# The mixer's values by seven block products instead of eight, all of them behind the second head's queries

## The chip, the cores and the metric

The kernel runs on one core of a Trainium2 chip. The metric is the device time of one execution in microseconds (us), the median of several runs. TensorE (PE) multiplies matrices, VectorE (DVE) and ScalarE (ACT) work on elements, GpSimd (POOL) and SyncE (SP) here mostly issue transfers. Each engine carries out its own instructions in order; engines wait for each other by semaphores.

## The reference

One transformer layer in fp32, for 512 tokens of width 1024: a gated feed-forward part (FFN1), the token mixer, a second feed-forward part (FFN2) and a final norm. The change is inside the mixer, in the projection that makes `va` and `vb`:

```python
def token_mixer(h, w_in, w_out, lq1, lk1, lq2, lk2, subln_gain, rel_bias, layer):
    proj = h @ w_in                                   # 512 x 1024 by 1024 x 3072
    qa, ka, va, qb, kb, vb = jnp.split(proj, ..., axis=-1)   # 512 columns each
    ...
    oa = diff_attention(qa, ka, va, lam, rel_bias[:, :2 * N_DIFF_HEADS])   # 4 heads of 128
    oa = rmsnorm(oa, subln_gain) * (1.0 - lam0)
    ...
    ob = dilated_attention(qb, kb, vb, rel_bias[:, 2 * N_DIFF_HEADS:])     # 8 heads of 64
    mixed = jnp.concatenate([oa, ob], axis=-1)
    return mixed @ w_out

def diff_attention(q, k, v, lam, bias_table):
    ...                                               # two causal softmaxes per head
    a = p[:, :, 0] - lam * p[:, :, 1]
    return a @ v
```

`h` is the normed input of the mixer. The values of the four differential heads are `va`, those of the eight dilated heads `vb`.

## The kernel before, in words

**Products.** Every matrix product in fp32 is made of three products in a faster format: an operand is split into a high part (a cast, on ACT) and a low part (operand minus high, on DVE), and `mm3` (L177) adds high by high, low by high and high by low. A product instruction takes 128 columns of a stationary operand and up to 512 columns of a moving one. The normed input stands transposed in eight pieces of 128 rows, high `xh` and low `xl`; their second 256 tokens are made later than the first, so some names end in m (`xh7m`).

**Stages.** FFN1, then the mixer, then FFN2. In both feed-forward parts block products are already done by seven products for eight; in the mixer no product is. The mixer's work on PE is cut into chunks of about six products of 512 columns. Its eight units u are the four differential heads (u = 0 to 3) and the eight dilated heads in pairs (u = 4 to 7). A list `plan` (L1381) names the blocks of chunks in order: `q0` stands for the queries and keys of unit 0 (eight chunks), `w` for the values of the four differential heads (16 chunks, `wide_chunks`, L1455: 96 products of 512 columns), `v2` and `v3` for the values of pairs of dilated units (eight chunks each, `v_chunks`, L1430: 96 products of 256 columns each). The order is q0 q1 w q2 q3 q4 v2 q5 q6 v3 q7, and then the output projection `wo`.

**Attention between the chunks.** `attention(u, s)` (L1598) hangs a unit's other work on chunk numbers with `put(chunk, rank, function)`: from chunk s the eight scores (L1616 and L1617, two maps of four tiles), each followed by a reduction with bias and minimum on DVE (L1619) and an exponential on ACT (L1622), then the combination of the two maps (L1626 to L1642), the turned weights (`pt`, L1652 and L1707, copied to `ptx` by ACT), the products with the values (`po`, L1691 and L1719), norm, scale (L1742), a last turn (`ot`, L1748) and the high and low parts for `wo` (`mh`, `ml`, L1754 to L1765). `step(t)` runs what was hung on chunk t with a rank below 10, then the chunk's products, then the rest.

**What sets the order.** PE's order is written by hand: as `step` issues it. On DVE, ACT, POOL and SP a scheduler sets it from priorities in the same sequence of issue. Weights come with `load_w` (L163) through SP; `prep` and `ahead` (L1414 and L1424) queue their casts (L1406) and lows (L1410) some chunks ahead.

**PSUM banks.** Score results use two banks (tag `s`), the turned weights two (tag `t`), products four (tag `mm`).

**Direct units.** A unit's keys and queries are needed in both halves of the 128 partitions. For units in `DIRECT` ACT and DVE write both halves (`evac_now`); for the others SP copies the other half by transfers (`evac_k`, L1532).

Of the kernel before, what the change touches and what calls it, by code (L numbers as in the profile page):

```python
# [37 lines left out]
DIRECT = (0, 7)  # L38
# [5 lines left out]
EARLY_SLOTS = {(1, 0): ((19, 20), (14, 15)), (1, 1): ((23, 0), (26, 27))}  # L44

# [72 lines left out]
def tile_macaron(ctx: ExitStack, tc, xs, xT, wf, wgu1, wst1, wdg1, wqk, wvw, wv, wo, wgu2, wst2,  # L118
# [1274 lines left out]
    def unit(src, nm):  # L1393
        units.append((src, nm))
        return len(units) - 1

    loaded, ready, later = {}, {}, []

    def load(n):
        if n < len(units) and n not in loaded:  # L1400
            loaded[n] = load_w(*units[n])
            ready[n] = loaded[n][1:]
# [20 lines left out]
    def ahead(n):  # L1423
        prep(n + 2)  # L1424
        load(n + 3)
        return ready[n]
# [3 lines left out]
    def v_chunks(qr):  # L1430
        vi, hf = qr // 2, qr % 2
        us = [unit(wv[hf, c], f"v{qr}{c}") for c in range(2)]
        st = {}

        def chunk(c):
            i, kh = c // 2, c % 2
            if c == 0:
                ahead(us[0])
            if kh == 0:
                st["ps"] = mm_bank(f"pv{qr}{i}")  # L1440
            po = st["ps"][:, :256]
            wh, wl = ready[us[kh]]
            xs = slice(i * P, (i + 1) * P)
            for k in range(4 * kh, 4 * kh + 4):
                o = (k % 4) * 256
                T.matmul(po, xh[k][:, xs], wh[:, o:o + 256], start=k == 0, stop=False)
                T.matmul(po, xl[k][:, xs], wh[:, o:o + 256], start=False, stop=False)
                T.matmul(po, xh[k][:, xs], wl[:, o:o + 256], start=False, stop=k == KD - 1)
            if kh == 1:
                if hf == 0:  # L1450
                    vt[vi, i] = slot(vi * 4 + i, f"v{vi}{i}")
                A.copy(vt[vi, i][:, hf * 256:hf * 256 + 256], po)
            if c == 7:
                ahead(us[1])
        return [lambda c=c: chunk(c) for c in range(2 * NQ)]  # L1455

    def wide_chunks():


        us = [unit(wvw[c], f"vw{c}") for c in range(4)]  # L1460
        banks = []

        def chunk(c, i):
            if i == 0:
                ahead(us[c])
            if c == 0:
                banks.append(mm_bank(f"pvw{i}"))
            po = banks[i][:]
            wh, wl = ready[us[c]]
            xs = slice(i * P, (i + 1) * P)  # L1470
            for k in range(2 * c, 2 * c + 2):
                o = slice(k % 2 * S, (k % 2 + 1) * S)
                T.matmul(po, xh[k][:, xs], wh[:, o], start=k == 0, stop=False)
                T.matmul(po, xl[k][:, xs], wh[:, o], start=False, stop=False)
                T.matmul(po, xh[k][:, xs], wl[:, o], start=False, stop=k == KD - 1)
            if c == 3:
                vt[0, i] = slot(i, f"v0{i}")
                A.copy(vt[0, i][:], po)
        return [lambda c=c, i=i: chunk(c, i) for c in range(4) for i in range(NQ)]
# [4 lines left out]
    def qk_chunks(u):  # L1484
# [3 lines left out]
        def chunk(k):  # L1488
            if k == 0:
                st["pq"] = mm_bank(f"pq{u}")  # L1490
                st["pk"] = mm_bank(f"pk{u}")
            if u == 4 and k == 0:

                load(us[0] + 3)
                put(start["q4"] + 3, 10, prep, us[0] + 2)
            elif k % 4 == 0:
# [101 lines left out]
    def attention(u, s):  # L1598
# [178 lines left out]
        if diff:  # L1777

            step, tv = (2, s + 13) if u > 1 else (1, v_end[u] + 1 + 3 * u)
# [8 lines left out]
            put(e + 3 + (u > 1), 9 if u < 2 else 7, scale)  # L1788
# [11 lines left out]
        else:  # L1800
            tv = max(s + 9, v_end[u])
# [8 lines left out]
    for w in plan:  # L1810
        if w == "w":
            chunks += wide_chunks()
            continue
        chunks += (qk_chunks if w[0] == "q" else v_chunks)(int(w[1]))
        if w[0] == "q":
            attention(int(w[1]), len(chunks) + (8 if w[1] == "0" else 3 if w[1] == "7" else 5))
# [32 lines left out]
    put(9, 4, lam)  # L1849
    for n, c in enumerate((0, 0, 2)):  # L1850
        put(c, 0, load, n)
    for n, c in enumerate((3, 5)):
        put(c, 10, prep, n)
# [179 lines left out]
_INS = ["xs", "xT", "wf", "wgu1", "wst1", "wdg1", "wqk", "wvw", "wv", "wo", "wgu2", "wst2", "wdg2", "fg",  # L2033
# [95 lines left out]
```

## Time and profile before

| | before |
|---|---|
| median of 3 runs (lowest, highest) | 912.9 us (912.56 to 913.06) |
| profiled execution, from its first to its last instruction | 910.7 us |
| its mean granted TensorE clock | 0.998 |
| PE, weight loads, DVE, ACT, POOL busy | 99%, 90%, 81%, 62%, 11% |
| the mixer's first products; first products of w, of v2, of wo | 339.0; 363.9; 436.3; 519.3 us |

The profile gives no time of its own for the profiled execution beside its span of 910.7 us; the median of the runs is 2.2 us above that. A row of a group of instructions holds the program's line, the engine, the operation, output and inputs, the shapes, the count, the busy time, the mean time of one in ns, and the idle time of the engine just before with what ended it. In a timeline a row begins with the start and the duration in us. In a table by windows each engine has its busy us, with the number of its instructions in brackets, then the granted clock, the share of the transfer engines and GB/s.

### The profile page before, as it was taken

What the parts mean: (1) busy time and instruction counts of PE and PEld (TensorE: products, weight loads), DVE (VectorE), ACT (ScalarE), POOL (GpSimd) and SP (SyncE); (2) the same over time, 40 slices, a digit from 0 to 9 for tenths busy, and PEclk for the clock granted to TensorE, in tenths of its full rate; (3) what the DMA queues carried; (4) which work ended last, traced back from release to release, by engine and by line L of the source; (5) the groups of instructions that cost most, each with busy time, mean ns of one, the idle gap of its engine ahead of it and who ended that gap; (6) DMA issues with size and microseconds to landing.
All of it is one profiled execution on the core that took longest, in us unless ns stands there. A gap on an engine that the chain in (4) does not pass through costs nothing.

```text
span 910.7 us, 16054 instructions
## 1 busy us (share of the span) xinstructions
PE 902.2 (99%) x5766; PEld 815.4 (90%) x5766; DVE 733.2 (81%) x1539; ACT 564.6 (62%) x1197; POOL 101.9 (11%) x127
## 2 busy tenths in 40 slices
PE   9999999999999999999999999999999999999996
PEld 7888998899998889888989778989999889999885
DVE  7798998889888886847875545888888888988995
ACT  7355675466667766656766675656666546666673
POOL 0001102121221100000000000011111112212200
PEclk9999999999999999999999999999999999999999
DMA  7454869587789712324333204364778669779902
GB/s 258 130 160 124 225 202 242 129 205 196 201 200 279 197 58 76 114 95 113 119 116 116 70 24 139 93 183 126 195 181 232 173 167 248 206 188 231 254 28 92
DMA packets 68544, 145.47 MB, mean 160 GB/s; under 512 B 7856, under 2 KB 8368, under 8 KB 68464
## 3 DMA queue, kind: packets, MB, share of 16 engines
q1 hardware_dynamic: 52032, 114.34, 38.3%
q0 software_dynamic: 16432, 30.11, 19.7%
q8 instruction: 45, 0.74, 0.3%
q14 instruction: 35, 0.29, 0.1%
HBM read 139.13 MB, written 2.14 MB: 155 GB/s over the span
## 4 chain that ended last, share of the span: by engine, by line
PE 98%; DVE 1%; ACT 0%; DMA 0%; issue 0%; DVEq 0%; SPq 0%; ACTq 0%
PE pt L178 8%; PE pt L180 8%; PE pt L179 8%; PE pq L178 2%; PE pwo L178 2%; PE pq L180 2%; PE pk L178 2%; PE pq L179 2%; PE pk L180 2%; PE pk L179 2%; PE pwo L180 2%; PE pwo L179 2%; PE pua L178 2%; PE pua L180 2%; PE pua L179 2%; PE pga L178 1%
## 5 line engine op out<-in xcount | busy, mean ns | idle before, releaser
L1622 ACT ACTIVATE pr<-pr,mx 128x128 f32<-128x128 f32 (+3 forms) x64 | 36.0, 563 | 36.7 <-DVE mx L1619 36.4
L1619 DVE CUSTOM_DVE_ANT_0 pr<-sc,strip 128x128 f32<-128x128 f32 (+3 forms) x64 | 30.5, 489 | 23.1 <-PE sc L1617 22.6
L551 DVE SCALAR_TENSOR_TENSOR x<-pt,x 128x512 f32<-128x512 f32 x50 | 33.2, 688 | 19.3 <-PE pt L180 12.1
L396 POOL DMA_DIRECT2D s1bg<-wst_dram x10 | 8.6, 862 | 329.0 <-DVE fin L1289 231.5
L457 DVE TENSOR_TENSOR w<-s2b,w 128x512 fp32r<-128x512 f32 x38 | 26.1, 686 | 8.1 <-ACT w L453 8.1
L453 ACT CAST w<-raa 128x512 fp32r<-128x512 f32 x34 | 20.9, 622 | 18.7 <-DVE raa L421 10.3
L453 ACT CAST w<-s2b 128x512 fp32r<-128x512 f32 x38 | 23.6, 620 | 7.9 <-DVE s2b L426 7.9
L453 ACT CAST w<-rab 128x512 fp32r<-128x512 f32 x28 | 17.3, 622 | 17.3 <-DVE rab L421 10.0
L178 PE MATMUL pwo<-w,mh 128*128 128x512 f32 x64 | 25.9, 405 | 0.0
L179 PE MATMUL pwo<-w,mh 128*128 128x512 f32 x64 | 25.0, 391 | 0.0
L180 PE MATMUL pwo<-w,ml 128*128 128x512 f32 x64 | 25.0, 391 | 0.0
L457 DVE TENSOR_TENSOR w<-s2a,w 128x512 fp32r<-128x512 f32 x30 | 20.6, 686 | 3.0 <-ACT w L453 2.9
L453 ACT CAST w<-s2a 128x512 fp32r<-128x512 f32 x30 | 18.6, 621 | 6.7 <-DVE s2a L426 5.9
L1410 DVE TENSOR_TENSOR w<-raw_qk,w 128x512 fp32r<-128x512 f32 x24 | 16.4, 687 | 7.9 <-ACT w L1406 7.8
L457 DVE TENSOR_TENSOR w<-raa,w 128x512 fp32r<-128x512 f32 x34 | 22.7, 684 | 0.0
L179 PE MATMUL pxgb<-ttb,w 128*128 128x256 f32 x80 | 22.5, 281 | 0.0
L396 POOL DMA_DIRECT2D s1ag<-wst_dram x8 | 7.1, 883 | 120.8 <-ACT xh L296 39.8
L1616 PE MATMUL sc<-k,q 128*128 128x128 f32 (+3 forms) x64 | 20.5, 322 | 0.0
L1617 PE MATMUL sc<-l,q 128*128 128x128 f32 (+3 forms) x64 | 20.2, 322 | 0.0
L179 PE MATMUL pxub<-ttb,w 128*128 128x256 f32 x72 | 20.2, 281 | 0.0
L457 DVE TENSOR_TENSOR w<-rab,w 128x512 fp32r<-128x512 f32 x28 | 18.7, 684 | 0.0
L179 PE MATMUL pwga<-xl,w 128*128 128x256 f32 x64 | 18.0, 281 | 0.0
(1135 smaller groups left out, 3917.8 us busy)
## 6 DMA issues: line engine op xcount, KB each, us to landing
raw_qk<-wqk_dram SPq DMA_DIRECT2D x12, 512.0 KB, 3.5
raw0bg<-wst_dram SPq DMA_DIRECT2D x10, 512.0 KB, 5.4
raw0bu<-wst_dram SPq DMA_DIRECT2D x9, 512.0 KB, 5.5
raw_gua<-wgu_dram SPq DMA_DIRECT2D x8, 512.0 KB, 3.7
raw0ag<-wst_dram SPq DMA_DIRECT2D x8, 512.0 KB, 4.4
strip<-bias_rows SPq DMA_DIRECT2D x16, 256.0 KB, 3.6
raw_wo<-wo_dram SPq DMA_DIRECT2D x8, 512.0 KB, 3.5
raw0au<-wst_dram SPq DMA_DIRECT2D x7, 512.0 KB, 5.8
```

Source lines behind the costliest of these rows:

```text
L178: T.matmul(po, wh, mh, start=first, stop=False, skip_group_check=on)
L179: T.matmul(po, wh, ml, start=False, stop=False, skip_group_check=on)
L180: T.matmul(po, wl, mh, start=False, stop=last, skip_group_check=on)
L396: nc.gpsimd.dma_start(t[:], b, accum_op=ALU.add)
L453: A.copy(made[t][0], source(t))
L457: V.tensor_tensor(l, source(t), h.bitcast(F32), op=ALU.subtract)
L551: V.scalar_tensor_tensor(o, a, f, b, op0=ALU.mult, op1=op1)
L1410: V.tensor_tensor(l[:, c:c + 512], raw[:, c:c + 512], h[:, c:c + 512].bitcast(F32), op=ALU.subtract)
L1616: T.matmul(ps[:, :w], qs[:, qi], ks[:, :w], start=True, stop=False)
L1617: T.matmul(ps[:, :w], qs[:, qi], ls[:, :w], start=False, stop=True)
L1619: V.tensor_tensor_reduce(out=pi, in0=ps[:, :w], in1=st["b"][m][:, w - 1::-1], op0=ALU.add, op1=ALU.min, scale=1.0, scalar=3.0e38, accum_ou ...
L1622: A.activation(pi, pi, AF.Exp, scale=-1.0, bias=st["mx"][:, m, i:i + 1], accum_out=st["ls"][:, m, i:i + 1])
```

## The change

The two value projections are one 1024 x 1024 projection now, in a block `V` behind q0 and q1, and w, v2 and v3 are gone. The matrix of weights and the turned input are each seen as two by two blocks, for each of four pairs p of 128-row pieces: `a11`, `a12` are the columns of `va`, `a21`, `a22` those of `vb`; `b11`, `b21` the first 256 tokens, `b12`, `b22` the others. Seven products of sums of blocks (`VALUE_SEVEN`) replace the eight of blocks: 7 x 4 pairs x 2 token blocks x 3 = 168 products of 512 columns, in 28 chunks.

- Sums of x, on DVE: `lefts` (8), `turned` (8), `turned_more` (4); their high parts on ACT (`turned_high`, 8), their low parts on DVE (`turned_low`, 8).
- Sums of weights: C = a21 + a22 and B = a11 + a21 by transfers that add, issued by POOL (8); s2 and s4 by `total` on DVE (8). The weights come through SP in 20 transfers of 256 KB; before it was 8 of 512 KB.
- Each of the 28 pieces of weights has its cast (`part_high`, ACT) and low part (`part_low`, DVE); before there were 16 of each.
- Products add into banks `w` (tag `s`), `v` and `z` (tag `mm`). Between them `result` copies banks (ACT, 10 copies) or subtracts (DVE, 4).
- Unit 0's scores start 25 chunks into V, unit 1's behind it; units 2 to 5 as before five chunks behind their own block, unit 6 and 7 at numbers of their own. There are 92 chunks ahead of wo; before there were 96. Unit 0 is no longer direct. The weights of q2 and q3 are fetched ahead by `fetch`.

```diff
-DIRECT = (0, 7)
+DIRECT = (7,)
+VALUE_SEVEN = (("a11", "w", "b11"), ("a12", "v", "b21"), ("s2", "w", "t2"), ("s3", "z", "t3"),
+               ("s1", "v", "t1"), ("a22", "w", "t4"), ("s4", "v", "b22"))
+VALUE_SLOTS = {"A": (2, 3, 12, 13), "F": (16, 17, 18, 21), "C": (4, 5, 6, 7), "B": (14, 15, 19, 20),
+               "E": (14, 15, 19, 20)}
...
-    plan = ["q0", "q1", "w", "q2", "q3", "q4", "v2", "q5", "q6", "v3", "q7"]
-    start = {w: 8 * i + 8 * (i > 2) for i, w in enumerate(plan)}
-    early_end = (11, 15)
-    v_end = [start["w"] + 16] * 4 + [start[f"v{u // 2}"] + 8 for u in range(4, 8)]
+    plan = ["q0", "q1", "V", "q2", "q3", "q4", "q5", "q6", "q7"]
+    start = {w: 8 * i + 20 * (i > 2) for i, w in enumerate(plan)}
+    early_end = (23, 41)
+    v_end = start["V"] + 4 * len(VALUE_SEVEN)
+    scored = {0: v_end - 3, 1: v_end + 5, 6: start["q6"] + 12, 7: start["q7"] + 13}
...
+        def load_part(n, p, *os):
+            dst = parts[n, p] = slot(VALUE_SLOTS[n][p], f"v{n}{p}")[:]
+            nc.sync.dma_start(dst, block(os[0], p))
+            for o in os[1:]:
+                nc.gpsimd.dma_start(dst, block(o, p), accum_op=ALU.add)
+        def total(o, p):
+            V.tensor_tensor(parts["A", p], parts["C" if o == "s2" else "F", p], parts["A", p], op=ALU.add)
...
+        def lefts(p):
+            for i, k in enumerate((2 * p, 2 * p + 1)):
+                V.tensor_tensor(t["y", p][:, i * HS:(i + 1) * HS], xh[k][:, left].bitcast(F32),
+                                xl[k][:, left].bitcast(F32), op=ALU.add)
...
+        def chunk(n, p):
+            o, b, blk = VALUE_SEVEN[n]
+            fresh = o in ("a11", "s3")
+            if fresh and p == 0:
+                bank(b)
+            h, l = made.pop((o, p))
+            bh, bl = stationary(blk, p)
+            for i in range(2):
+                c = slice(i * P, (i + 1) * P)
+                mm3(banks[b][i], bh[:, c], bl[:, c], h, l, fresh and p == 0, p == 3, not fresh)
+        def result(o):
+            if o == "a11":
+                bank("v")
+            for i in range(2):
+                w, v, z = [banks[b][i] if b in banks else None for b in "wvz"]
+                if o == "a11":
+                    A.copy(v, w)
+                elif o == "a12":
+                    vt[0, i] = slot(i, f"v0{i}")
+                    A.copy(vt[0, i][:], v)
+                elif o == "s2":
+                    A.copy(v, w)
+                elif o == "s3":
+                    vt[1, i] = slot(4 + i, f"v1{i}")
+                    A.copy(vt[1, i][:], z)
+                elif o == "s1":
+                    vt[1, 2 + i] = slot(6 + i, f"v1{2 + i}")
+                    V.scalar_tensor_tensor(vt[1, 2 + i][:], v, -1.0, vt[1, i][:], op0=ALU.mult, op1=ALU.subtract)
+                elif o == "a22":
+                    V.scalar_tensor_tensor(vt[1, i][:], w, -1.0, vt[1, i][:], op0=ALU.mult, op1=ALU.subtract)
+                else:
+                    vt[0, 2 + i] = slot(2 + i, f"v0{2 + i}")
+                    A.copy(vt[0, 2 + i][:], v)
+        for p in range(4):
+            put(p, 0, load_part, "A", p, "a11")
+            put(p + 2, 0, load_part, "F", p, "a12")
+            put(p + 6, 0, load_part, "C", p, "a21", "a22")
+            put(13 + p // 2, 10, load_part, "B", p, "a11", "a21")
+            put(v0 + 10 + p, 10, load_part, "E", p, "a22")
...
+        for n, (o, b, blk) in enumerate(VALUE_SEVEN):
+            for p in range(4):
+                c = v0 + 4 * n + p
+                if o in ("s2", "s4"):
+                    put(c - 5, 7.4, total, o, p)
+                put(c - 4, 7.6, part_high, o, p)
+                put(c - 3, 7.5, part_low, o, p)
+            put(v0 + 4 * n + 4, 0, result, o)
```

**How it moves instructions.** First PE, from the last products of q1 on. In an instruction's row the output stands before the arrow and the inputs behind it; `sc010` is unit 0, map 1, tile 0; `pvw` and `pv` are the banks of values, `pq`, `pk` those of queries and keys. Before:

```order
L179 MATMUL pk1_3872<-xl7m_3754,wqh11512_3853 128x256
L180 MATMUL pk1_3872<-xh7m_3753,wql11512_3854 128x256
L1616 MATMUL sc000_4097<-k00_4013,q00_4011 128x128
L1617 MATMUL sc000_4097<-l00_4015,q00_4011 128x128
L1473 MATMUL pvw0_4106<-w_105,xh0_78 128x512
L1474 MATMUL pvw0_4106<-w_105,xl0_86 128x512
L1475 MATMUL pvw0_4106<-w_105,xh0_78 128x512
L1473 MATMUL pvw0_4106<-w_105,xh1m_3747 128x512
L1474 MATMUL pvw0_4106<-w_105,xl1m_3748 128x512
L1475 MATMUL pvw0_4106<-w_105,xh1m_3747 128x512
L1616 MATMUL sc010_4120<-k10_4014,q10_4012 128x128
```

and with the change:

```order
L185 MATMUL pk1_3902<-xl7m_3754,wqh11512_3870 128x256
L186 MATMUL pk1_3902<-xh7m_3753,wql11512_3871 128x256
L184 MATMUL pvw0_4135<-w_105,xh0_78 128x512
L185 MATMUL pvw0_4135<-w_105,xh0_78 128x512
L186 MATMUL pvw0_4135<-w_105,xl0_86 128x512
L184 MATMUL pvw1_4136<-w_105,xh0_78 128x512
L185 MATMUL pvw1_4136<-w_105,xh0_78 128x512
L186 MATMUL pvw1_4136<-w_105,xl0_86 128x512
L184 MATMUL pvw0_4135<-w_105,xh2_80 128x512
L185 MATMUL pvw0_4135<-w_105,xh2_80 128x512
L186 MATMUL pvw0_4135<-w_105,xl2_88 128x512
```

The scores of unit 0, which stood two by two between the products of values from the first on, are gone from here; V's products follow each other, a stationary piece of x for three of them, two banks in turn.

Second DVE, in the same stretch of the program: before, at the place where the queries and keys of units 0 and 1 are split and unit 0's first scores reduced (L1513, L1195, L1619):

```order
L1195 TENSOR_TENSOR l00_4015<-pk0_3775,k00_4013 64x512
L1513 SCALAR_TENSOR_TENSOR q10_4012<-pq0_3774,q10_4012 64x512
L1195 TENSOR_TENSOR l10_4016<-pk0_3775,k10_4014 64x512
L1619 ISA pr00_4045,mx0_4047<-sc000_4097,strip0_4041 128x128
L1619 ISA mx0_4047 128x1
L1195 TENSOR_TENSOR l01_4093<-pk1_3872,k01_4091 64x512
L1195 TENSOR_TENSOR l11_4094<-pk1_3872,k11_4092 64x512
L1619 ISA pr01_4046,mx0_4047<-sc010_4120,strip1_4043 128x128
L1619 ISA mx0_4047 128x1
L1513 SCALAR_TENSOR_TENSOR q01_4089<-pq1_3871,q01_4089 64x512
L1513 SCALAR_TENSOR_TENSOR q11_4090<-pq1_3871,q11_4090 64x512
L1410 TENSOR_TENSOR w_105<-raw_vw2_3826,w_105 128x512
```

and with the change, where V's first weights are split (`vA`, `vF` are weights, L1201 their low parts, `vx`, `vt` sums of x):

```order
L1504 SCALAR_TENSOR_TENSOR vx3_3852<-xt13_3876,x0_104,vx3_3852 128x256
L1524 SCALAR_TENSOR_TENSOR vt01_3889<-vx0_3846,vt00_3888 128x512
L1201 TENSOR_TENSOR w_105<-vA0_3770,w_105 128x512
L1201 TENSOR_TENSOR w_105<-vA1_3812,w_105 128x512
L1524 SCALAR_TENSOR_TENSOR vt11_3893<-vx1_3848,vt10_3892 128x512
L1201 TENSOR_TENSOR w_105<-vA2_3828,w_105 128x512
L1201 TENSOR_TENSOR w_105<-vA3_3844,w_105 128x512
L1524 SCALAR_TENSOR_TENSOR vt_tx_4059<-vx2_3850,vt_tx_4059 128x512
L1201 TENSOR_TENSOR w_105<-vF0_3826,w_105 128x512
L1201 TENSOR_TENSOR w_105<-vF1_3842,w_105 128x512
L1524 SCALAR_TENSOR_TENSOR vt_tx_4059<-vx3_3852,vt_tx_4059 128x512
L1466 TENSOR_TENSOR vA0_3770<-vC0_3943,vA0_3770 128x512
```

The first reduction (L1619 before, L1737 now) has moved from row 576 of DVE to row 649; sums of x and their low parts, sums of weights (L1466) and low parts of weights stand there instead.

Third PE where unit 4's block of queries begins. Before, v2 followed it, and unit 3's scores stood between products of 256 columns (`pv20`):

```order
L180 MATMUL pk4_4672<-xh7m_3753,w_105 128x512
L1707 MATMUL pt23_4814<-ident_96,pr20_4578 128x128 x4
L1616 MATMUL sc311_4825<-k13_4656,q13_4654 128x256
L1617 MATMUL sc311_4825<-l13_4658,q13_4654 128x256
L1446 MATMUL pv20_4834<-w_105,xh0_78 128x256
L1447 MATMUL pv20_4834<-w_105,xl0_86 128x256
L1448 MATMUL pv20_4834<-w_105,xh0_78 128x256
L1446 MATMUL pv20_4834<-w_105,xh1m_3747 128x256
```

With the change q4 follows q3, and unit 2's scores stand between the products of queries and keys:

```order
L1825 MATMUL pt13_4830<-ident_96,pr10_4527 128x128 x4
L1734 MATMUL sc211_4841<-k12_4631,q12_4629 128x256
L1735 MATMUL sc211_4841<-l12_4633,q12_4629 128x256
L184 MATMUL pq4_4848<-xh0_78,w_105 128x512
L185 MATMUL pq4_4848<-xl0_86,w_105 128x512
L186 MATMUL pq4_4848<-xh0_78,w_105 128x512
L184 MATMUL pk4_4849<-xh0_78,w_105 128x512
L185 MATMUL pk4_4849<-xl0_86,w_105 128x512
L186 MATMUL pk4_4849<-xh0_78,w_105 128x512
L1866 MATMUL ot0_4865<-ident_96,ob0_4727 128x128 x4
L1734 MATMUL sc202_4873<-k02_4630,q02_4628 128x384
L1735 MATMUL sc202_4873<-l02_4632,q02_4628 128x384
```

From q2 to q7 each unit's eight chunks now hold one unit's scores, turned weights, values and last turn, with no chunk of values between the units.

More of the change, by code (lines that the diff above doesn't have):

```diff
@@ L1428, in tile_macaron @@
     vt = {}
[L1430 to L1455, printed above, removed]
@@ L1491, in chunk @@
                 st["pk"] = mm_bank(f"pk{u}")
[L1492 to L1496, printed above, removed]
+            if k % 4 == 0:
                 ahead(us[k // 4])
@@ L1777, in attention @@
         if diff:
-            step, tv = (2, s + 13) if u > 1 else (1, v_end[u] + 1 + 3 * u)
+            step, tv = 2 if u else 1, s + 13
             put(tv - 2 - step, 2, turn, ((0, 2), (1,)))
@@ L1787, in attention @@
                 put(e + 2 + j // 2, 8, lambda j=j: st["rs"][j]())
-            put(e + 3 + (u > 1), 9 if u < 2 else 7, scale)
+            put(e + 4, 7, scale)
             put(e + 6, 3, finish)
```

140 lines of the change are left out of this document (102 added, 38 removed).

## The prediction

> **What bounds the kernel now.** I read the totals and the chain of waits first, then a table of the mixer by windows, then the waits, then single rows.
>
> ```profile
> PE 902.2 (99%) x5766; PEld 815.4 (90%) x5766; DVE 733.2 (81%) x1539; ACT 564.6 (62%) x1197; POOL 101.9 (11%) x127
> PE 98%; DVE 1%; ACT 0%; DMA 0%; issue 0%; DVEq 0%; SPq 0%; ACTq 0%
> ```
>
> PE is busy 902.2 of 910.7 us and is 98% of the chain that ended last. So a PE product that goes is time that goes, as long as nothing makes PE wait. The mixer by stages (q0 and q1; w; the stretch from q2 to v2; v2; the rest; the start of wo), then twelve dense us inside v2, then a stretch of FFN1:
>
> ```profile
> core 0: us, PE busy (x) PEld busy (x) DVE busy (x) ACT busy (x) POOL busy (x), PEclk, DMA share, GB/s
> 339.00:363.70 24.70, 24.70 (x209) 24.70 (x208) 16.14 (x44) 15.70 (x35) 0.57 (x1) 1.00 0.22 70
> 363.70:391.50 27.80, 27.64 (x137) 23.08 (x136) 22.22 (x75) 19.40 (x51) 0.00 (x0) 1.00 0.38 114
> 391.50:436.20 44.70, 44.70 (x241) 38.17 (x240) 29.93 (x91) 24.88 (x67) 0.00 (x0) 1.00 0.36 107
> 436.20:460.00 23.80, 23.80 (x187) 23.01 (x186) 17.32 (x60) 16.36 (x46) 0.00 (x0) 1.00 0.37 111
> 460.00:519.30 59.30, 59.30 (x359) 49.99 (x358) 38.35 (x111) 38.69 (x96) 0.00 (x0) 1.00 0.35 107
> 519.30:545.00 25.70, 25.70 (x140) 19.42 (x139) 11.79 (x35) 19.34 (x48) 0.00 (x0) 1.00 0.06 21
> 440.00:452.00 12.00, 12.00 (x100) 11.82 (x100) 10.51 (x38) 7.81 (x27) 0.00 (x0) 1.00 0.38 108
> 140.00:304.00 164.00, 164.00 (x1126) 152.84 (x1125) 141.98 (x256) 100.35 (x206) 33.40 (x40) 1.00 0.81 212
> ```
>
> In all of the mixer PE lacks 0.16 us, at the full clock. DVE and ACT are busy some 65% of it, and they wait for PE, not PE for them:
>
> ```profile
> ACT pr L1622 <- DVE mx L1619: 35.4, 33, 3.7
> DVE pr L1619 <- PE sc L1617: 22.6, 23, 2.8
> ```
>
> **The change: what PE does less.** Products are counted by the distance of their starts, since their durations overlap:
>
> ```profile
> 385.34 0.39 PE L1473 MATMUL pvw<-w,xh 128*128 128x512 f32 x1
> ...
> 387.83 0.39 PE L1475 MATMUL pvw<-w,xh7m 128*128 128x512 f32 x1
> ...
> 436.28 0.28 PE L1446 MATMUL pv<-w,xh 128*128 128x256 f32 x1
> ...
> 437.71 0.34 PE L1616 MATMUL sc<-k,q 128*128 128x384 f32 x1
> ```
>
> Between the first two stand 11 steps of 512 columns: 2.49 / 11 = 0.226 us. Between the last two stand 12 products of 256 columns: 1.43 / 12 = 0.119 us. With a first step after a change of shape counted in I take 0.228 and 0.119. Before: 96 x 0.228 + 192 x 0.119 = 21.9 + 22.8 = 44.7 us. After: 168 x 0.228 = 38.3 us. The saving is **6.4 us**. Its bounds: 0.232 for V's products, were they dearer with their other stationary pieces, while w's stay at 0.228, gives 5.7; 0.226 for both gives 6.5. All other products of the mixer stay as many as they were.
>
> [...]
>
> **What DVE and ACT do more.** The nearest rows for the new work:
>
> ```profile
> L1410 DVE TENSOR_TENSOR w<-raw_vw,w 128x512 fp32r<-128x512 f32 x8 | 5.4, 684 | 0.0
> L1285 DVE SCALAR_TENSOR_TENSOR xl<-xt,x,xh 128x256 fp32r<-128x256 f32 x7 | 3.3, 478 | 0.3 <-ACT xh7m L1283 0.3
> L1762 DVE SCALAR_TENSOR_TENSOR ml<-ot,sub,mh 128x512 fp32r<-128x512 f32 x4 | 3.0, 751 | 0.1
> L1406 ACT CAST w<-raw_vw 128x512 fp32r<-128x512 f32 x8 | 4.8, 614 | 0.0
> L1478 ACT COPY v<-pvw 128x512 f32<-128x512 f32 x4 | 2.4, 596 | 0.8 <-PE pvw L1475 0.8
> ```
>
> DVE: 28 lows of weights instead of 16, 12 x 0.684 = 8.2; sums of x, 16 of 256 columns by 0.478 = 7.6 (0.42 of a reduction of that width would make it 6.8) and 4 by 0.684 = 2.7; 8 lows of x and 8 sums of weights, 16 x 0.684 = 10.9; four results from PSUM, 4 x 0.751 = 3.0. Together +32 us, on 135.8 us of busy time in the first six windows: about 168 of 200 us. ACT: 12 more casts and 8 high parts by 0.614 = 12.3, ten copies instead of four long and eight short ones about -2 to +1: +12 us on 134, far from full. So DVE goes from 66% to some 84% of the mixer, and whether PE then waits is the question of this case. I go through it by place.
>
> **The start of V.** The first product of V needs the lows of its first weights.
>
> ```profile
> 345.16 0.49 DVE L1244 TENSOR_SCALAR y<-x,fin 128x512 f32<-128x512 f32 x1
> 346.95 0.69 DVE L1195 TENSOR_TENSOR wql<-raw_q,wqh 128x512 fp32r<-128x512 f32 x1 [1.30 <-ACT wqh L1192]
> 347.56 1.28 DVE L1410 TENSOR_TENSOR w<-raw_vw,w 128x512 fp32r<-128x512 f32 x2
> 348.76 0.48 DVE L1285 SCALAR_TENSOR_TENSOR xl<-xt,x,xh 128x256 fp32r<-128x256 f32 x1
> 349.15 0.47 DVE L1285 SCALAR_TENSOR_TENSOR xl1m<-xt,x,xh1m 128x256 fp32r<-128x256 f32 x1
> ```
>
> Dense DVE work goes by distances shorter than the durations: 0.60 us for a low of 512 columns (two start and end within 1.28, the next starts 1.20 after the first), 0.39 for 256 columns. From 345.6 on DVE has 8 sums, one low, 8 lows of x, seven numbers of about 0.2, 8 more sums, one low of x and the first weights: 8 x 0.39 x 3 + 0.6 x 3 + 1.4 = 12.6 us, so the first low is there at 358.2, and the second at 359; V begins at 363.7. Cover 5 us; cost nothing. Without that cover each late us is one of PE's. Inside V, DVE's 28 lows, 8 sums and the rest are about 31 us at these distances against 38.3 us of PE: it gains ground.
>
> **Seams of V.** The products of a12 add on to a copy of a11's bank. Behind a bank's last product stand three products of the other bank, 0.68 us; the copy is 0.60 and starts when the last product ends, 0.39 after its start. So PE waits about 0.60 + 0.39 - 0.23 - 0.68 = 0.1 us and two semaphores; I take **0.3** (bounds 0 and 0.6, the whole copy). At s2's copy s3 stands between, four chunks of 1.37 us: nothing.
>
> **Weights.** The pieces A, F and C find their places free before q0 and are there. B goes where q1's weights were, last read 36 (B2, B3) and 24 products (B0, B1) ahead of V: free at 363.7 - 36 x 0.119 = 359.4 and 360.8. It comes by SP and then a transfer that adds, on POOL:
>
> ```profile
> raw_vw<-wvw_dram SPq DMA_DIRECT2D x4, 512.0 KB, 3.9
> sBa<-wdg_dram POOLq DMA_DIRECT2D x11, 256.0 KB, 7.0
> s1ag<-wst_dram POOLq DMA_DIRECT2D x8, 256.0 KB, 4.3
> ```
>
> 360.8 + 3.9 + 7.0 = 371.7, and about 1 us later for the last of four; PE wants it in chunk 12 of V, 363.7 + 12 x 1.37 = 380.1, ACT four chunks before, at 374.7. Covered by 2 to 3 us for ACT, by 8 for PE. If it came late, ACT's copy of s2 and the casts of later pieces would stand behind the waiting cast. E waits until the lows of B are done (about 379), and needs 3.9; PE wants it at 391. POOL's eight issues stand on an engine with nothing else to do here.
>
> **Units 2 to 5 without chunks of values between them.** Before, PE's time per unit held more chunks than a unit's own; now each has 48 x 0.228 = 10.9 us of queries and keys and its attention: the third window holds 24 chunks of 1.37, 32.9 us, and for about two units 11.8 us of attention, 5.9 each; with the last turn I take 6.2 and 17.1 us. DVE per differential unit: 4 lows of weights, 4 of 64 rows, 8 reductions, 4 combinations, scale, low and about 25 small ones:
>
> ```profile
> L1513 DVE SCALAR_TENSOR_TENSOR q<-pq,q 64x512 fp32r<-64x512 f32 x14 | 9.6, 689 | 5.2 <-ACT q L1510 4.8
> L1195 DVE TENSOR_TENSOR l<-pk,k 64x512 fp32r<-64x512 f32 x14 | 9.6, 689 | 7.6 <-ACT k L1192 7.4
> L1410 DVE TENSOR_TENSOR w<-raw_qk,w 128x512 fp32r<-128x512 f32 x24 | 16.4, 687 | 7.9 <-ACT w L1406 7.8
> L1619 DVE CUSTOM_DVE_ANT_0 pr<-sc,strip 128x512 f32<-128x512 f32 x14 | 9.6, 688 | 1.6 <-PE sc L1617 1.5
> L1619 DVE CUSTOM_DVE_ANT_0 pr<-sc,strip 128x384 f32<-128x384 f32 x14 | 7.8, 556 | 7.3 <-PE sc L1617 7.1
> L1619 DVE CUSTOM_DVE_ANT_0 pr<-sc,strip 128x256 f32<-128x256 f32 x14 | 5.9, 423 | 7.0 <-PE sc L1617 6.9
> L1619 DVE CUSTOM_DVE_ANT_0 pr<-sc,strip 128x128 f32<-128x128 f32 x14 | 4.0, 289 | 7.2 <-PE sc L1617 7.1
> ```
>
> Lows 2.7, 64 rows 2.8, reductions 3.9 with 0.7 for reading their minima, combinations of the same four widths 2.2, scale and low 1.4, small ones 4.2: **17.9 us by durations, 15.8 by distances** (92% of PE's 17.1). Dilated pairs cost less. The nearest row for such density is 440 to 452, where DVE is busy 10.51 of 12 us and PE 12.00. So I take **0.4** in all for moments where a reduction frees a score's bank late; bounds 0, and 4 x (17.9 - 17.1) = 3.2.
>
> **The end.** Unit 7's scores start five chunks into wo, not three. Before, 24 products stand behind its values and ahead of the first product that needs them, now 12: 2.7 us, against a cast and a low of about 1.3. **0.3** (bounds 0 and 0.6). Unit 0's four more transfers run on SP while V runs: nothing.
>
> Sum: 910.7 - 6.4 + 0.3 + 0.4 + 0.3 = 905.3 us for the span, and 2.2 us around it as before: **907.5 us**.
>
> **Rivals.** *DVE at its durations* in units 2 to 5: +2.8 on the forecast, **910.3**. For it: 751 ns from PSUM does not shrink much; against it: the distances. *DVE's waits stay (the slower side).* Before, DVE waits 22.6 us ahead of its reductions, 5.2, 7.6 and 7.9 ahead of L1513, L1195 and the weights' lows: 43.3 us or 5.4 per unit. If these come not from DVE's being early but from the chain of score, reduction, exponential and combination, in an order that DVE can't change, then 15.8 + 5.4 = 21.2 stands against 17.1. It decides from 1.3 us of idle time per unit; the kernel gets slower than before from 2.7 (four units); with three quarters of it, 2.75 x 4 = 11 on 907.1: **918**. Against it: those waits end with PE's scores, so a PE that comes earlier shortens them. [...] *The gain is handed back* at V's seams, with a sixth of a us at each of its 28 new pieces and the first of them late: 6.4 - 28 x 0.17 - 1 = 0.6, **912.3**, no change. PE's gaps of 0.16 us in the mixer speak against it.
>
> **How the numbers follow.** Forecast 0.70, DVE at its durations 0.11, its waits 0.10, starved transfers 0.04, handed back 0.05. A measurement of this kernel tells 0.2%, 1.8 us: faster is below 911.1, slower above 914.7. Faster: 0.69 of the forecast's 0.70 and 0.09 of the second's 0.11: 0.78. Same: 0.02 of the second, the fifth's 0.05, 0.01 each of the third and fourth: 0.09. Slower: the rest, 0.13. The likeliest case's own range is 906.2 (saving 6.5, no small term, 0.2 of a wait gone) to 909.4 (saving 5.7, seams and end at 0.6, one us for banks). For 8 in 10 it goes 0.3 lower for the measurement's own spread, 912.56 to 913.06, and up through the second case to the fifth: **905.9 to 912.0**.
>
> **What would show it.** Products in V 0.226 to 0.232 us apart, 168 of them, 38 to 39 us from V's first to its last; no wait of PE at V's first product; one or two of 0.3 us at a12's first. DVE busy 165 to 170 us in the mixer and no PE wait above half a us for a reduction's bank between q2 and q6. B landed by 374. The order would be wrong if PE's waits named DVE's reductions in every unit (third case), or POOL's transfers in V (fourth).

## The result and the profile after

The changed kernel takes 907.76 us (907.22 to 908.14, four runs) where the kernel before, run beside it, takes 912.73 us (912.36 to 913.06). The ratio is 0.9937, with a 95% interval of 0.9923 to 0.9952: 5.0 us faster. The profiled execution took 907.75 us, with a span of 906.0; before, the span was 910.7. One execution, the profiled one of the kernel with one more low (below), ran at a granted clock of 0.217 and took 3912 us; it is left out of that kernel's median, and there is no other profile of it.

The totals and the chain of waits of the changed kernel:

```profile
PE 897.2 (99%) x5646; PEld 805.9 (89%) x5646; DVE 759.6 (84%) x1591; ACT 573.5 (63%) x1211; POOL 109.2 (12%) x135
PE 96%; DVE 2%; ACT 1%; issue 0%; DMA 0%; DVEq 0%; SPq 0%; ACTq 0%
```

PE still sets the end. It has 120 instructions fewer, as counted (288 products gone, 168 come), and DVE is busy 26 us longer (32 us of instructions were worked out; their durations overlap: two of 0.68 us start at 364.56 and 365.16). Where in the span the 4.7 us went is read from four rows, the first product of q0 and the last product of wo, of the kernel before:

```profile
339.00 0.28 PE L178 MATMUL pq<-xh,wqh 128*128 128x256 f32 x1
...
574.61 0.39 PE L180 MATMUL pwo<-w,ml 128*128 128x512 f32 x1
```

and of the changed one:

```profile
339.46 0.28 PE L184 MATMUL pq<-xh,wqh 128*128 128x256 f32 x1
...
570.13 0.39 PE L186 MATMUL pwo<-w,ml 128*128 128x512 f32 x1
```

The mixer went from 235.61 to 230.67 us: 4.94 us less. Ahead of it 0.46 us were lost (below, under what had not been expected), behind it 0.22 gained; together 4.7.

Inside the mixer, the block V begins like this in the timeline of PE:

```profile
364.20 0.40 PE L184 MATMUL pvw<-w,xh 128*128 128x512 f32 x1
...
369.44 0.39 PE L186 MATMUL pvw<-w,xl 128*128 128x512 f32 x1
369.81 0.50 PE L184 MATMUL pvv<-w,xh1m 128*128 128x512 f32 x1
```

24 products of a11 stand 5.24 / 23 = 0.228 us apart. The first product of a12 comes 0.37 behind, so the copy between the two banks costs 0.14 us. From 364.20 to q2's first product at 403.62 are 39.42 us: 38.3 for 168 products, 0.14 for this copy, and 0.9 to 1.0 for the four pairs of scores in it.

After V the table by blocks of queries, q2 to q7:

```profile
core 0: us, PE busy (x) PEld busy (x) DVE busy (x) ACT busy (x) POOL busy (x), PEclk, DMA share, GB/s
403.62:419.25 15.63, 14.86 (x77) 12.29 (x75) 12.71 (x41) 10.09 (x28) 0.00 (x0) 1.00 0.44 134
419.25:436.27 17.02, 17.02 (x96) 14.53 (x95) 14.42 (x49) 12.11 (x35) 0.00 (x0) 1.00 0.39 115
436.27:453.56 17.29, 17.29 (x100) 15.00 (x99) 15.56 (x54) 12.44 (x37) 0.00 (x0) 1.00 0.41 121
453.56:470.87 17.31, 17.31 (x101) 14.93 (x100) 15.58 (x54) 12.46 (x37) 0.00 (x0) 1.00 0.46 123
470.87:489.38 18.51, 18.51 (x110) 15.89 (x109) 16.35 (x56) 15.02 (x42) 0.00 (x0) 1.00 0.44 127
```

PE is busy without a gap in the blocks of q3 to q6, at 17.0 to 17.3 us for a differential unit (17.1 were worked out). DVE is busy 15.56 of 17.29 us there. All the waits of PE in the mixer are two rows:

```profile
PE sc L1734 <- DVE mx L1737: 0.8, 1, 0.8
PE pt L1770 <- DVE pr L1756: 0.4, 1, 0.4
```

The first is in block q2, ahead of unit 0's sixth score; by the starts of the products it costs 0.93 us. The second is ahead of unit 6's last turned weights at 519.97, a pause of 0.55 us. With the seam of 0.14 the three make 1.6 us. 44.7 us of products before, less 38.3 (168 at 0.228 us), less 1.6, is 4.8 us of gain; 4.94 were measured, so 0.1 us between them stays open.

The two rows of waits that the prediction showed of before have shrunk on the other side, where DVE and ACT wait:

```profile
ACT pr L1740 <- DVE mx L1737: 25.9, 26, 2.0
...
DVE pr L1737 <- PE sc L1735: 4.4, 7, 1.1
```

DVE waited 22.6 us for scores before and waits 4.4 now: most of its new work went into pauses in which it had waited for PE.

### The profile page after: what moved, and what is told of

It is laid out like the page before. It is cut to its first block, busy times and chain, and to the rows that moved or that the text cites. A ratio compares the mean times of both kernels' runs of the same rounds, so it can differ in the third digit from the quotient of the medians.

```text
span 906.0 us, 15970 instructions
## 1 busy us (share of the span) xinstructions
PE 897.2 (99%) x5646; PEld 805.9 (89%) x5646; DVE 759.6 (84%) x1591; ACT 573.5 (63%) x1211; POOL 109.2 (12%) x135
## 4 chain that ended last, share of the span: by engine, by line
PE 96%; DVE 2%; ACT 1%; issue 0%; DMA 0%; DVEq 0%; SPq 0%; ACTq 0%
PE pt L186 8%; PE pt L184 8%; PE pt L185 8%; PE pq L184 2%; PE pq L185 2%; PE pq L186 2%; PE pk L184 2%; PE pk L186 2%; PE pk L185 2%; PE pua L184 2%; PE pua L186 2%; PE pua L185 2%; PE pwo L184 1%; PE pwo L186 1%; PE pwo L185 1%; PE pga L184 1%
## 5 line engine op out<-in xcount | busy, mean ns | idle before, releaser
L1737 DVE CUSTOM_DVE_ANT_0 pr<-sc,strip 128x128 f32<-128x128 f32 (+3 forms) x64 | 30.6, 487 | 7.2 <-PE sc L1735 6.7
L459 ACT CAST w<-rab 128x512 fp32r<-128x512 f32 x28 | 17.3, 622 | 17.8 <-DVE rab L427 9.5
```

The costliest lines, as they stand in the source:

```text
L459: A.copy(made[t][0], source(t))
L1737: V.tensor_tensor_reduce(out=pi, in0=ps[:, :w], in1=st["b"][m][:, w - 1::-1], op0=ALU.add, op1=ALU.min, scale=1.0, scalar=3.0e38, accum_ou ...
```

## The experiments

### Eight products in the same place

All values in one block at V's place, with the scores at their distances, but with eight products of plain blocks, no sums and no adding transfers. The core of the edit:

```diff
-    start = {w: 8 * i + 20 * (i > 2) for i, w in enumerate(plan)}
-    early_end = (23, 41)
-    v_end = start["V"] + 4 * len(VALUE_SEVEN)
+    start = {w: 8 * i + 24 * (i > 2) for i, w in enumerate(plan)}
+    early_end = (23, 45)
+    v_end = start["V"] + 32
...
-        def chunk(n, p):
-            o, b, blk = VALUE_SEVEN[n]
...
+        def chunk(o, p, side):
...
+            k = 2 * p + (not top)
+            for n in range(2):
+                c = slice(side * HS + n * P, side * HS + (n + 1) * P)
+                mm3(banks[vi, side][n], xh[k][:, c], xl[k][:, c], h, l, first, last)
...
+        turns = [(o, p) for o in ("a11", "a12", "a21", "a22") for p in range(4)]
```

> The values of all heads in one block behind the second unit's queries, as in the changed kernel, but by eight products of plain blocks: 32 chunks, 192 products of 512 columns, no sums of x or of weights, no transfers that add, 16 casts and 16 lows of weights. All scores keep their distance from the end of the block and from their own blocks. Theory A (the changed kernel's time is its PE products and a few short waits): 24 more products at 0.229 us, +5.5 us, less 0.14 us for the copy between a11 and a12, so 913.2 us, between 912.4 and 914.0; against the kernel before this is no change, so that the seventh product makes all of the gain. Theory B (VectorE's 32 us of new work costs PE some us in the block): then the eight products, without that work, give less than 5.5 us away, 909 to 911.5 us. The wait of 0.8 us at unit 0's scores stays by A's reading of it (unit 1's queries and keys are split just there) and goes if the block's own work on VectorE makes it.

Measured: 912.15 us, a ratio to the kernel before of 0.9992 (0.9982 to 1.0003), 4.4 us above the changed kernel. Its waits of PE:

```profile
PE pq L184 <- ACT v L1485: 0.6, 1, 0.6
PE pt L1668 <- DVE pr L1654: 0.4, 1, 0.4
```

The first of them is of this kernel's own making: the last copies of values free the bank of q2's queries late, 0.8 us by the starts. The block of values, from its first product to q2's first, takes 45.31 us against 39.42, so 5.9 us more: 5.5 for the 24 products and 0.8 for this wait, less 0.14 for the copy between a11 and a12, make 6.2, and 0.3 us stay open. Block q2 takes 14.71 us against 15.63, because PE's wait at unit 0's scores is not there. From q0's first product to wo's last it takes 235.73 us, where the kernel before took 235.61 and the changed kernel 230.67.

The time lies just under A's range, and by these spans A is right on what makes most of the gain: going from eight products to seven gives 5.06 us, 4.3 when this kernel's own wait is taken off (5.5 for the products, less waits of 0.14 and 0.93, is 4.4). One block and moved scores by themselves give nothing that a measurement tells. The wide instructions should save 0.9 us by the prediction's distances (its 22.8 us of products of 256 columns become 21.9); this kernel does not show it, since its two waits, 0.8 and some 0.5 us, take as much. B is right on the wait: V's own work on DVE makes it, since unit 1's split stands at the same place in both kernels. The 32 us of DVE work cost PE 0.9 us out of 5.5.

### DVE's room between q2 and q6

The prediction gave DVE 1.3 us of room per unit. Three kernels test it from above, by making one, two or four of a unit's four lows of weights twice in the blocks q2 to q5, and one from below, by leaving out two of them there (that one's queries and keys are then not exact). The edits, for two more and two fewer (one more has ((0, 0),) in place of the pair, four more all four combinations):

```diff
     def low(n, c):
         raw, h, l = loaded[n]
         V.tensor_tensor(l[:, c:c + 512], raw[:, c:c + 512], h[:, c:c + 512].bitcast(F32),
                         op=ALU.subtract)
+        if 2 <= n <= 9 and (n % 2, c) in ((0, 0), (1, 0)):
+            V.tensor_tensor(l[:, c:c + 512], raw[:, c:c + 512], h[:, c:c + 512].bitcast(F32),
+                            op=ALU.subtract)
```

```diff
     def low(n, c):
         raw, h, l = loaded[n]
+        if 2 <= n <= 9 and c == 512:
+            return
```

> The changed kernel, with two of the four lows of weights that VectorE makes per unit made twice during the blocks q2 to q5: +1.2 us of VectorE work per unit by the distance of 0.60 us, +1.4 us by the duration of 0.69 us, in four units. Theory A (15.8 us of VectorE work by distances against 17.1 us of PE per unit, 1.3 us of room): 0 to +0.8 us in all, 907.8 to 908.6 us. Theory B (VectorE at its durations, 17.9 us against 17.1 us, so that VectorE already sets the pace): +1.2 to 1.4 us per unit, 912.6 to 913.4 us. Theory C (waits of VectorE in its order stay, so that any work added shows): +2 to +5 us.

> The changed kernel, with all four lows of weights that VectorE makes per unit made twice during the blocks q2 to q5: +2.4 us of VectorE work per unit by distances, in four units. Theory A (1.3 us of room per unit): (2.4 - 1.3) x 4 = +4.4 us, 912.2 us, and PE's waits name VectorE's reductions or lows. Theory B (no room): +9.6 us or more, 917.4 us. If the room is larger than worked out, less than +2 us, below 909.8 us.

> The changed kernel with one of the four lows of weights per unit made twice during the blocks q2 to q5: +0.7 us of VectorE work per unit (a repeated low on the same tile starts 0.72 us behind the first). With two repeats the four blocks took 17.4, 18.4, 18.9 and 20.0 us instead of 17.0, 17.3, 17.3 and 18.5. Theory A as forecast (1.3 us of room per unit) is out by that; theory A' (VectorE's dense work with its waits for ScalarE is 17 to 17.5 us per unit, so that it stands level with PE's 17.3): +0.4 to 0.7 us in the blocks of q4, q5 and q6 each, +1.2 to 2.2 us in all, 909.0 to 910.0 us. Theory C (the price of two repeats comes from the place of the second one, not from the amount): 0 to +0.5 us.

> The changed kernel with two of the four lows of weights per unit left out during the blocks q2 to q5 (the products there read what the place held before, so the queries and keys of four units lose their exactness): 1.2 us less VectorE work per unit. Theory A' (PE sets the pace of these blocks in the changed kernel, VectorE stands just under it): no change, 907.4 to 908.0 us, blocks of 17.0 and 17.3 us as they are. Theory B (VectorE already sets the pace): -1 us per unit, 903.5 to 905 us.

| lows per unit more or fewer | median us | against the changed kernel | per unit | q0's first to wo's last product, us |
|---|---|---|---|---|
| -2 | 908.13 | +0.4 | +0.1 | 230.50 |
| 0 | 907.76 | | | 230.67 |
| +1 | 909.59 | +1.8 | +0.5 | no profile |
| +2 | 912.92 | +5.2 | +1.3 | 235.68 |
| +4 | 919.41 | +11.7 | +2.9 | 241.51 |

A repeated low costs 0.72 us of DVE's time, not the 0.60 between independent ones: it starts 0.72 us behind the first, which writes the same tile and has ended 0.04 us before, as two rows of the kernel with four more show:

```profile
439.18 0.68 DVE L1426 TENSOR_TENSOR w<-raw_qk,w 128x512 fp32r<-128x512 f32 x1
439.90 0.69 DVE L1429 TENSOR_TENSOR w<-raw_qk,w 128x512 fp32r<-128x512 f32 x1
```

So one more per unit has a price of 0.72 us and costs 0.5, two have 1.44 and cost 1.3, four have 2.88 and cost 2.9 by the medians (2.7 by the last column, which leaves out what differs ahead of the mixer). Work taken away gains next to nothing, 0.17 us in the last column: the blocks of q3 to q6 last 17.04, 17.29, 17.29 and 18.37 us with two fewer, against 17.02, 17.29, 17.31 and 18.51. The kink lies at the changed kernel itself: PE sets the length of the blocks there, and DVE has no room for one low more.

All theories missed in part. A's room of 1.3 us is wrong. B's times were met with two and with four more (912.6 to 913.4; 917.4 or more), but its mechanism, DVE at 17.9 us by durations, does not hold: the blocks would be 17.9 us long in the changed kernel, and two fewer would gain 1 us each. C, that the place of the second repeat decides, gave at most 0.5 us for one more, and 1.8 were measured. A' was formed after the kernels with two and four more. It met its range for one more, though the blocks that it named for that kernel were not measured; for two fewer the median is 0.1 us above its range, and the blocks are as it said.

Where PE waits with two more, and the blocks q4, q5 and q6 of that kernel, in the columns of the table above:

```profile
PE pk L184 <- DVE ob L1863: 3.4, 3, 1.3
```

```profile
438.62:457.02 18.40, 17.61 (x100) 14.80 (x99) 16.65 (x53) 12.63 (x36) 0.00 (x0) 1.00 0.40 114
457.02:475.95 18.93, 17.60 (x100) 14.79 (x99) 17.12 (x55) 12.62 (x36) 0.00 (x0) 1.00 0.40 112
475.95:495.98 20.03, 18.70 (x111) 15.90 (x110) 17.79 (x63) 15.17 (x42) 0.00 (x0) 1.00 0.40 117
```

It is not a reduction that PE waits for but the scale (`ob`, L1860 in the changed kernel), which frees the bank of an older unit's values for the keys of the next block: once per block, at its second group of products. In the changed kernel, the first three of these scales and the products that take their banks are:

```profile
435.87 0.69 DVE L1860 TENSOR_TENSOR ob<-po,f 128x512 f32<-128x512 f32 x1
453.33 0.69 DVE L1860 TENSOR_TENSOR ob<-po,f 128x512 f32<-128x512 f32 x1
470.80 0.69 DVE L1860 TENSOR_TENSOR ob<-po,f 128x512 f32<-128x512 f32 x1
```

```profile
436.96 0.39 PE L184 MATMUL pk<-xh,w 128*128 128x512 f32 x1
454.25 0.39 PE L184 MATMUL pk<-xh,w 128*128 128x512 f32 x1
471.56 0.49 PE L184 MATMUL pk<-xh,w 128*128 128x512 f32 x1
```

The first scale ends at 436.56, so 0.40 us are to spare; at the second it is 0.23, at the third 0.07. The scales come 17.46 and 17.47 us apart, PE's products 17.29 and 17.31: DVE is already slower than PE by 0.2 us per unit, and only the 0.40 us that the first scale had to spare keep that out of the time until the differential units end (the next scale, begun at 487.93, has 1.5 us to spare). With two lows fewer the scales come 17.16 and 17.29 us apart and 1.0 to 1.1 us stay to spare.

With four more, the table and DVE's waits in block q4:

```profile
438.84:459.24 20.40, 17.81 (x100) 14.77 (x99) 18.51 (x58) 12.62 (x36) 0.00 (x0) 1.00 0.35 104
```

```profile
DVE f L1856 <- ACT ob L1848: 0.6, 1, 0.6
DVE l L1201 <- ACT k L1198: 0.4, 1, 0.4
```

DVE is busy 18.51 of 20.40 us; 1.0 us are two waits for ACT, and the other 0.9 lie, by the rows of the changed kernel, between small instructions that need each other's results: there such a one starts 0.03 to 0.04 us behind the end of the last. 20.40 less 2.88 is 17.5 us: that is what a differential unit asks of DVE, as the distances of the scales in the changed kernel say too, and not 15.8.

### Unit 1's split at another place

The wait in block q2 stands behind DVE's splits of unit 1's queries and keys. In DVE's timeline of the changed kernel:

```profile
404.30 1.39 DVE L1631 SCALAR_TENSOR_TENSOR q<-pq,q 64x512 fp32r<-64x512 f32 x2
405.73 0.69 DVE L1426 TENSOR_TENSOR w<-raw_qk,w 128x512 fp32r<-128x512 f32 x1
406.34 0.16 DVE L1744 RECIPROCAL rl<-ls 128x2 f32<-128x2 f32 x1
406.53 0.22 DVE L1747 SCALAR_TENSOR_TENSOR cc<-ls,nlam,rl 128x1 f32<-128x1 f32 x1
406.79 0.35 DVE L1751 SCALAR_TENSOR_TENSOR pr<-pr,cc,pr 128x128 f32<-128x128 f32 x1
407.17 0.42 DVE L1737 CUSTOM_DVE_ANT_0 pr<-sc,strip 128x256 f32<-128x256 f32 x1
```

The score that this last row reduces was issued at 403.38; 2.9 us of other work stand ahead of its reduction, and PE, which needs the bank at 406.7, waits until 407.66. Two kernels move the split:

```diff
-    early_end = (23, 41)
+    early_end = (23, 33)
```

```diff
-    early_end = (23, 41)
+    early_end = (17, 23)
```

> The changed kernel with one number changed: unit 1's queries and keys are split eight chunks earlier, in the middle of the values' block instead of at unit 0's first scores. Theory A: VectorE's four instructions for it (two of 1.4 us each by pairs) and ScalarE's four no longer stand between unit 0's reductions, the wait of PE for a reduction (0.8 us before the score at 407.66 us) goes, and VectorE has room for them in the block: 907.0 us, 906.4 to 907.6. Theory B (VectorE is behind at the end of the block, whatever stands there): the wait stays or moves into the block, 907.6 to 909.

Measured: 907.87 us, ratio 0.9939 (0.9921 to 0.9957). DVE now made the split at 389 to 393 us, and PE waited as long as before, elsewhere:

```profile
PE sc L1734 <- DVE v L1570: 0.8, 1, 0.8
```

L1570 is the last result of V that DVE takes out of bank w, which unit 0's first score needs. B was right.

> The changed kernel with the queries and keys of units 0 and 1 split earlier in the block of values (chunks 18 to 19 and 24 to 25 instead of 24 to 25 and 42 to 43). When unit 1's split went from chunk 42 to 34, VectorE did it at 389 to 393 us, and PE's wait of 0.8 us only went from unit 0's fifth score to its first, which then waited for the last results of the block. VectorE pauses 2.7 us between 366 and 377 us in the changed kernel and 1.3 us between 387 and 391. If the wait is VectorE's lack of time behind 389 us alone, work done before 377 takes it away: 907.0 us. If the block's weights and sums are already paced by VectorE from its beginning, the wait stays or grows: 907.8 to 909 us.

Measured: 907.32 us, ratio 0.9937 (0.9923 to 0.9950), 0.4 us below the changed kernel, which the intervals don't tell from nothing, and between the times of the two readings. Block q2 takes 14.59 us, as in the kernel with eight products, but there is a new wait inside V, for a low of a weight:

```profile
PE pvz L185 <- DVE w L1201: 0.7, 1, 0.7
```

Mixer against mixer, 230.55 us stand against 230.67. The lag of DVE is handed on, not lost: in all three places of the split, with unit 0's scores where they were, 0.7 to 0.8 us of DVE's work come too late for PE between 377 and 407 us.

### First scores one chunk later

```diff
-    scored = {0: v_end - 3, 1: v_end + 5, 6: start["q6"] + 12, 7: start["q7"] + 13}
+    scored = {0: v_end - 2, 1: v_end + 5, 6: start["q6"] + 11, 7: start["q7"] + 13}
```

> The changed kernel with two numbers changed: unit 0's first scores one chunk later (26 chunks into the block of values), unit 6's one chunk earlier. If the wait of 0.8 us in block q2 comes from VectorE being behind at the end of the block of values, one chunk more (1.4 us) lets it catch up and the wait goes; if the wait of 0.4 us for unit 6's last scaled weights (the pause of 0.55 us at 519 us) comes from their being asked for too early, it goes too: 906.4 to 906.9 us. If VectorE's lag is only handed on to the next scores, 907.5 to 908.5 us.

Measured: 909.63 us, ratio 0.9970 (0.9959 to 0.9980), 1.9 us slower than the changed kernel: a miss. Block q2 took 14.43 us, so that wait went, but PE's waits were now:

```profile
PE pk L184 <- DVE ob L1860: 2.1, 1, 2.1
PE pt L1770 <- DVE pr L1756: 0.9, 1, 0.9
```

The whole of unit 0 had moved by a chunk, and its scale came 2.1 us late for the keys of q4 (block 19.75 us, the same place where additional lows had hurt). Unit 6's earlier scores made its wait longer. The next kernel moves unit 0's scores alone, and leaves unit 6:

```diff
-    scored = {0: v_end - 3, ...
+    scored = {0: v_end - 2, ...
...
-            step, tv = 2 if u else 1, s + 13
+            step, tv = 2 if u else 1, s + 13 - (u == 0)
```

> The changed kernel with unit 0's first scores one chunk later, and its turned weights, values, norm and scale at the chunks where they were. When all of unit 0 went one chunk later, the wait of 0.8 us in block q2 went and a wait of 2.1 us for unit 0's scale came at pk of q4, whose bank the scale frees. If that is the whole reason, both waits are away now: block q2 14.5 us, q3 17.1, q4 17.3, and 906.9 us (906.3 to 907.4). If unit 0's turned weights are now asked for before VectorE has combined them, PE waits there instead: 907.5 to 908.5 us.

Measured: 906.82 us in the median, ratio 0.9936 (0.9923 to 0.9950). Blocks 15.42, 17.07, 17.28 and 17.29 us, and the waits:

```profile
PE pt L1770 <- DVE pr L1756: 0.4, 1, 0.4
PE pt L1825 <- DVE rl L1744: 0.4, 1, 0.4
```

The scale is in time again, but unit 0's turned weights are asked for before DVE has combined them, as the second reading said; the time is the first one's. The mixer takes 230.23 us, 0.44 less than in the changed kernel. The median is the lowest of all, 0.9 us below the changed kernel's, but the intervals of the two ratios are nearly the same, so the 0.9 us are not told from nothing, and the mixer's 0.44 us are one profile against one.

### B's loads later

```diff
-            put(13 + p // 2, 10, load_part, "B", p, "a11", "a21")
+            put(21 + p // 2, 10, load_part, "B", p, "a11", "a21")
```

> The changed kernel with the four loads of B = a11 + a21 (SyncE's and then GpSimd's adding transfer) issued eight chunks later, inside the block of values: about 371 us instead of 360. In the changed kernel B's last piece is issued at 366.2 us and landings take 4.4 us, its first cast is at 377.3 us and its first product at 380.84 us. Forecast's reading (cover by landing times, nothing starved): SyncE's part lands at 375, the adding one at about 380 to 381.5, cast and low take 1.3 us, so PE waits 1 to 3 us at the first products of s3: 908.8 to 911 us. If adding transfers starve while VectorE is dense (5.5 of 5.5 us at 381 to 386), PE waits 8 us or more: above 915 us.

Measured: 907.71 us, ratio 0.9941 (0.9926 to 0.9956). It tells nothing on the question: SP issued B's loads at 359.8 to 361.6 us, as in the changed kernel (360.0 to 361.8), so their later place in the program did not hold them back. The kernel is a second measurement of the changed one. What there is on starved transfers stands in the changed kernel's own rows for B:

```profile
L1460 POOL DMA_DIRECT2D vB<-wvd_dram x4: 857/982/1106, 363.3 to 366.2; - x4
L1198 ACT CAST w<-vB x4: 614/618/627, 377.3 to 380.2; 128x512 fp32r<-128x512 f32 x4
...
DMA to landing us min/median/max: 2.8/4.4/6.7
```

The last row is over SP's and POOL's eight. In 364.2 to 369.7 us DVE was busy 4.90 of 5.50 us, and no landing took more than 6.7. The 0.04 for starved transfers rests on an assumption of the author, that adding transfers are held up while DVE is dense; the landings show no stall, and no run shows one.

## Why the prediction was right

It gave 907.5 us, faster, and 907.76 was measured. By its steps:

- **PE's products**: 38.3 us for V's, and 0.228 us between their starts were measured. Of the 6.4 us, 5.5 are the seventh product, and the kernel with eight products shows them, less the waits that they cost; the other 0.9 are the wide instructions, which no run shows by themselves. The distance that the prediction took from the trace before, 0.228 us, holds in the changed kernel too.
- **The start of V**: the first low of V's weights was worked out for 358.2 us; DVE started it at 358.42. The second came at 360.33 where 359 was said, after 1.2 us of waiting for ACT's cast; the cover held, and PE's first product at 364.20 waited for nothing.
- **Seams**: 0.3 us taken, 0.14 measured.
- **Weights**: B by 374 us was said; its last transfer was issued at 366.2, so with the longest landing, 6.7, it was there by 373, and ACT asked for it at 377.3. No PE wait names a transfer.
- **Inside V**: "it gains ground" did not hold to V's end. About 31 us of DVE's work were worked out against 38.3 of PE; DVE was busy 33.96 of V's 39.42 us, and behind V the reduction that unit 0's sixth score needs came 0.93 us late, which did not happen in the kernel without V's sums. That breaks the sign "no PE wait above half a us for a reduction's bank between q2 and q6".
- **Units 2 to 5**: 0.4 us were taken for banks freed late, and the units as such cost nothing. The time was right, and the reason given for it only in part: "92% of PE's 17.1" is the step that failed. The sum by distances, 15.8 us, is DVE's busy time (15.56 were measured), but a unit asks 17.5 us of it, with 0.9 to 1.0 us of waits for ACT's squares and casts and the rest between dependent small instructions. Those were no slack that other work could use at this place: with four more lows the two waits stood there as before, 0.6 and 0.4 us against 0.5 and 0.4. The room was not 1.3 us but less than nothing, 0.2 us per unit, and that it cost no time was luck: the third scale had 0.07 us to spare. One more low per unit cost 1.8 us.
- **The end**: 0.3 us for unit 7, where nothing was lost; 0.55 us at unit 6's turned weights, which the prediction did not name.

The three small terms came to 1.6 us where 1.0 was taken, and the span to 906.0 us where the sum gave 905.3. The 2.2 us around the span were too many: they are 1.8 in the changed kernel (907.75 less 906.0). So it is partly luck that the time missed by only 0.3 us.

Of the rivals, DVE at its durations was refuted by the blocks of 17.0 to 17.3 us, starved transfers by B's landings, and the gain handed back by V's seam of 0.14 us. Of DVE's waits, those for scores went, from 22.6 to 4.4 us; but this third case, which "decides from 1.3 us of idle time per unit", was nearer than its chance of 0.10: with 1.7 us idle per unit (15.73 of the 17.46 us from scale to scale were busy) DVE was past PE's 17.29.

## What to carry to other kernels

PE was busy throughout here, and a product of 512 columns that went was worth its distance to the next, 0.228 us, less the waits that the change made: 5.5 us for the seventh product, less 1.1. Work added to DVE was nearly free where it fell into pauses in which DVE waited for PE: V's 32 us of it cost PE 0.9. How much more DVE could take was not the sum of its instructions, 15.8 us, against PE's 17.3: its waits for a third engine (0.9 us a unit) and the gaps between dependent instructions (0.8) counted as work, and the first place to break was the one instruction that frees a bank, the scale with 0.07 us to spare. Before trusting a margin, read from stage to stage how far apart that instruction comes and what it has to spare, or add one instruction per stage and look for the kink.

## What had not been expected of the hardware

The first products of FFN1 run at one of two distances. Before:

```profile
5.60 0.40 PE L1132 MATMUL pua<-eha,w 128*128 128x512 f32 x1
5.84 0.40 PE L1132 MATMUL pga<-eha,w 128*128 128x512 f32 x1
```

and in the kernel with two lows fewer:

```profile
6.12 0.63 PE L1138 MATMUL pua<-eha,w 128*128 128x512 f32 x1
6.55 0.63 PE L1138 MATMUL pga<-eha,w 128*128 128x512 f32 x1
```

0.24 and 0.43 us apart. The slow ones last until 6.7 us in the changed kernel (four products) and until 10.3 in this one (eleven products, and its q0 begins at 341.45 us instead of 339.46), although the program is the same up to there. This is where the 0.46 us ahead of the mixer went: the first product of `pga` behind this stretch starts at 8.15 us before and at 8.61 in the changed kernel. So the profiled spans are compared from the mixer's first product on. What makes the two distances, no run shows: the table by windows has a granted clock of 1.00 for 5 to 7 us of the changed kernel, where the slow products stand.
